# Four triangular inverses of a delta-rule layer: their 31 steps on GpSimd in place of VectorE

## The chip, the core and the metric

The kernel runs on one core of a Trainium2 chip. The metric is the device time of one execution in microseconds (us). Three runs of the kernel before gave 2785.96, 2793.25 and 2799.57 us, so a median of 2793.25 us.

## The reference

The program computes two blocks one after the other on 256 tokens of 1024 channels. The first is a stack of two layers, each with latent attention, a gated convolution, a sparse attention and a feed-forward network. The second block mixes differential attention with a delta-rule recurrence that runs over a context of 256 tokens and then over the 256 tokens themselves, forwards and backwards, in 16 heads of 64 channels; a feed-forward part of 16384 small experts follows. What the change touches is the recurrence. The reference writes it token by token:

```
def step(s, inp):
    w, kk, a, k, v, r = inp
    sa = jnp.einsum('dbhij,dbhj->dbhi', s, kk)
    s = s * w[..., None, :] - sa[..., :, None] * (kk * a)[..., None, :] + v[..., :, None] * k[..., None, :]
    return s, jnp.einsum('dbhij,dbhj->dbhi', s, r)
```

## The kernel before, in words

Every weight matrix is read in float32 pieces (tile `raw`, loads on the SP queue, line 304). ScalarE rounds a piece to `wh` (line 312), VectorE forms the rest `wl = raw - wh` (the subtraction helper, line 277), and TensorE multiplies with both halves (lines 333 to 335 and 351 to 353). This runs through nearly the whole program. There are three or four buffers of `wh` and `wl` each, so a split can be a few pieces ahead of the matmuls.

The recurrence is cut into chunks of 32 tokens. Inside a chunk the delta rule is a triangular system, and `wkv_front` inverts all its 32 x 32 matrices at once: 128 of them, one per partition (2 chunks of a pair, 2 directions, 32 combinations of pair and head). The function is called four times, once for each half of the heads and for context and tokens: in layer 1 and layer 2 of the first block beside the feed-forward network (for the context), in the second block beside the projections of the attention (tokens, first half) and beside the differential attention (tokens, second half). I call them the first to fourth inverse, and their places stretches 1 to 4.

One inverse goes like this. The masked products `ML` (tile `w8`) are stored in DRAM (`din`, lines 1313 and 1314) and loaded again with one matrix per partition as `Bt` (line 1316). `X` starts as minus the identity (memsets of lines 1318 and 1319). Then 31 steps follow, k = 0 to 30: a product of k+1 rows by 31-k columns into `tmp`, and its subtraction from `X`. Both are written with helpers, so that the profile shows them under line 271 (`mul`) and line 277 (`sub`), as tiles `w`; each step needs the one before it. `X` is stored (`dout`, line 1327) and loaded back in two layouts (lines 1331 and 1332), and the half that belongs to one direction is transposed on VectorE in 32 x 32 blocks (line 1333). First to use the inverse is the matmul of line 1392 in `wkv_back`, the part that runs through the chunks one after the other.

The order of the instructions of each engine is set when the program is built: a scheduler simulates the program with costs of its own and puts an instruction in its engine's queue where it expects its inputs to be there, calls of `wkv_front` and `wkv_back` ahead of other work that is ready. On the chip each queue then runs strictly in that order. An instruction whose input is late holds up all that stand behind it.

Of the kernel before, what the change touches and what calls it, by code (L numbers as in the profile page):

```python
# [15 lines left out]
ALU = mybir.AluOpType  # L16
# [178 lines left out]
class Kern:  # L195
# [980 lines left out]
    def wkv_front(self, pool, src, hf, zd, wa, own=False):  # L1176


        nc, C, P = self.nc, self.C, self.P2
# [135 lines left out]
        Bt = self.w4(pool, [128, 32, 32])  # L1315
        nc.sync.dma_start(Bt, din.rearrange("c d k r s -> (c d k) r s"))
        X = self.w4(pool, [128, 32, 32])
        nc.gpsimd.memset(X, 0.0)
        nc.vector.memset(X.rearrange("p a b -> p (a b)")[:, 0::33], -1.0)
        tmp = self.w4(pool, [128, 1024])  # L1320
        for k in range(31):
            n = 31 - k
            p = tmp[:, :(k + 1) * n].rearrange("p (c s) -> p c s", s=n)
            self.mul(p, X[:, 0:k + 1, k:k + 1].to_broadcast([128, k + 1, n]), Bt[:, k + 1:, k].unsqueeze(1).to_broadcast([128, k + 1, n]))
            self.sub(X[:, 0:k + 1, k + 1:], X[:, 0:k + 1, k + 1:], p)
        dout = self.t(self.dram, [2, 2, 32, 32, 32], "dout", bufs=2)
        nc.sync.dma_start(dout.rearrange("c d k r s -> (c d k) r s"), X)
        TB = self.w4(pool, [128, 32, 32])
# [624 lines left out]
```

## Time and profile before

| | |
|---|---|
| median of 3 runs | 2793.25 us |
| profiled execution | 2798.71 us, span 2796.9 us |
| TensorE busy | 2635.9 us, 94% of the span |
| VectorE busy | 1978.4 us, 71% |
| ScalarE busy | 1423.3 us, 51% |
| GpSimd busy | 14.2 us, 1% |

PE is TensorE's matmuls, PEld its weight loads, DVE is VectorE, ACT is ScalarE, POOL is GpSimd, SP issues the loads and stores. A busy share is a mean over stages that have different limits, so the four stretches of the inverses are read by themselves.

### The profile page before, as it was taken

The page shows a single profiled execution, that of the slowest core. Times are in us where ns is not written, and L with a number is a line of the kernel's source. Part 1 is how long each engine was busy: PE and PEld are TensorE (multiplying, and loading weights), DVE is VectorE, ACT ScalarE, POOL GpSimd, SP SyncE. Part 2 cuts the span into 40 slices and gives each one's busy share as a digit, 9 for nine tenths or more (in the row PEclk, how much of TensorE's full clock was granted, in tenths as well). Part 3 has the DMA queues.
Part 4 walks back from the last instruction along what each step waited for, and adds up shares of the span by engine and source line. Part 5 has one row for each costly group of instructions (what it writes and reads, how often), then busy time and mean ns, then how long its engine had stood idle before and what let it go on. Part 6 is the DMA issues. An engine that isn't in the chain of part 4 may idle for free.

```text
span 2796.9 us, 54976 instructions
## 1 busy us (share of the span) xinstructions
PE 2635.9 (94%) x21856; PEld 2293.4 (82%) x21856; DVE 1978.4 (71%) x4085; ACT 1423.3 (51%) x2392; POOL 14.2 (1%) x45
## 2 busy tenths in 40 slices
PE   7999899999999999987998979989989999999999
PEld 7986588886997768877888755779989998888887
DVE  5996668765897658766788776566987765666665
ACT  4554446543555446534664655444446554444444
POOL 0000000000000000000000000000000000000000
PEclk9999999999999999988999976699999999999999
DMA  5532866546543555535746522264664346666665
GB/s 189 175 124 88 263 225 199 168 152 219 167 147 126 162 199 170 173 107 166 237 134 200 166 68 59 67 200 163 190 185 137 122 149 208 215 208 219 207 216 183
DMA packets 212433, 472.00 MB, mean 169 GB/s; under 512 B 52816, under 2 KB 86480, under 8 KB 211152
## 3 DMA queue, kind: packets, MB, share of 16 engines
q1 hardware_dynamic: 212176, 468.48, 52.4%
q8 instruction: 172, 2.82, 0.4%
q14 instruction: 85, 0.70, 0.1%
HBM read 427.77 MB, written 40.63 MB: 167 GB/s over the span
## 4 chain that ended last, share of the span: by engine, by line
PE 79%; DVE 10%; DMA 6%; ACT 4%; issue 2%; SPq 0%; DVEq 0%; ACTq 0%
PE a L333 8%; PE a L335 8%; PE a L334 8%; PE b L353 4%; PE b L351 4%; PE b L352 4%; PE b L1767 3%; PE x L335 3%; PE x L333 3%; PE x L334 3%; PE a L352 3%; PE a L351 3%; PE a L353 3%; DVE wl L277 3%; DMA raw<-in_peer 2%
## 5 line engine op out<-in xcount | busy, mean ns | idle before, releaser
L312 ACT ACTIVATE wh<-raw 128x1024 fp32r<-128x1024 f32 (+1 forms) x701 | 638.2, 913 | 689.3 <-PE a L334 247.4
L277 DVE TENSOR_TENSOR wl<-raw,wh 128x1024 fp32r<-128x1024 f32 (+1 forms) x701 | 727.4, 1041 | 357.9 <-ACT wh L312 332.6
L333 PE MATMUL a<-hh,wh 128*128 128x256 f32 x1920 | 550.2, 287 | 8.8 <-ACT hh L1621 4.1
L335 PE MATMUL a<-hh,wl 128*128 128x256 f32 x1920 | 549.5, 286 | 4.5 <-DVE wl L277 4.2
L334 PE MATMUL a<-hl,wh 128*128 128x256 f32 x1920 | 547.2, 285 | 0.6 <-DVE hl L277 0.5
L333 PEld LDWEIGHTS a<-hh,wh 128*128 128x128 f32 x1920 | 365.5, 190 | 22.0 <-ACT wh L312 4.9
L335 PEld LDWEIGHTS a<-hh,wl 128*128 128x128 f32 x1920 | 365.2, 190 | 14.8 <-DVE wl L277 9.0
L334 PEld LDWEIGHTS a<-hl,wh 128*128 128x128 f32 x1920 | 364.9, 190 | 5.4 <-DVE hl L277 0.7
L333 PE MATMUL x<-hh,wh 128*128 128x256 f32 x720 | 205.8, 286 | 5.6 <-ACT wh L312 5.2
L335 PE MATMUL x<-hh,wl 128*128 128x256 f32 x720 | 206.6, 287 | 3.0 <-DVE wl L277 3.0
L334 PE MATMUL x<-hl,wh 128*128 128x256 f32 x720 | 204.9, 285 | 0.0
L352 PE MATMUL b<-wl,ah 128*128 128x512 f32 x512 | 201.0, 393 | 0.0
L351 PE MATMUL b<-wh,ah 128*128 128x512 f32 x512 | 191.2, 393 | 2.8 <-issue 2.8
L353 PE MATMUL b<-wh,al 128*128 128x512 f32 x512 | 191.8, 391 | 0.0
L333 PEld LDWEIGHTS x<-hh,wh 128*128 128x128 f32 x720 | 137.2, 191 | 9.0 <-ACT wh L312 6.7
L335 PEld LDWEIGHTS x<-hh,wl 128*128 128x128 f32 x720 | 136.9, 190 | 5.7 <-DVE wl L277 4.4
L1802 ACT ACTIVATE ah<-pact 128x256 fp32r<-128x256 f32 x128 | 52.6, 412 | 173.1 <-PE b L352 160.3
L334 PEld LDWEIGHTS x<-hl,wh 128*128 128x128 f32 x720 | 137.1, 190 | 0.8
L352 PE MATMUL a<-wl,hh 128*128 128x256 f32 (+2 forms) x416 | 128.6, 309 | 8.0 <-DVE wl L277 7.9
L351 PE MATMUL a<-wh,hh 128*128 128x256 f32 (+2 forms) x416 | 125.3, 308 | 6.2 <-DVE hl L395 3.9
L277 DVE TENSOR_TENSOR wl<-rawv,wh 128x1024 fp32r<-128x1024 f32 x84 | 101.7, 1222 | 37.1 <-ACT wh L312 37.0
L353 PE MATMUL a<-wh,hl 128*128 128x256 f32 (+2 forms) x416 | 125.9, 304 | 0.0
(672 smaller groups left out, 5436.7 us busy)
## 6 DMA issues: line engine op xcount, KB each, us to landing
raw<-in_flat SPq DMA_DIRECT2D x289, 512.0 KB, 4.0
raw<-in_peer SPq DMA_DIRECT2D x172, 512.0 KB, 3.9
raw<-in_flat SPq DMA_DIRECT2D x228, 256.0 KB, 3.6
rawv<-in_peer SPq DMA_DIRECT2D x84, 512.0 KB, 4.6
TG<-in_flat SPq DMA_DIRECT2D x52, 512.0 KB, 5.9
parked<-act SPq DMA_DIRECT2D x89, 128.0 KB, 2.1
pact<-parked SPq DMA_DIRECT2D x89, 128.0 KB, 4.5
w<-vtd SPq DMA_DIRECT2D x32, 128.0 KB, 4.1
```

Source lines behind the costliest of these rows:

```text
L277: self.nc.vector.tensor_tensor(out, a, b, op=ALU.subtract)
L312: self.nc.scalar.activation(h, src, AF.Copy)
L333: mm(ps, wh[:, k], xh[:, k], start=first and k == 0, stop=False)
L334: mm(ps, wh[:, k], xl[:, k], start=False, stop=False)
L335: mm(ps, wl[:, k], xh[:, k], start=False, stop=last and k == nk - 1)
L351: mm(ps, xh[:, k], wh[:, k], start=first and k == 0, stop=False)
L352: mm(ps, xh[:, k], wl[:, k], start=False, stop=False)
L353: self.last = mm(ps, xl[:, k], wh[:, k], start=False, stop=last and k == nk - 1)
L1767: nc.tensor.matmul(ps[:, c], a[:, n, g, :, c], b[:, g, :, c], start=n == 0, stop=n == 2)
L1802: nc.scalar.activation(ah, act, AF.Copy)
```

## The change

The memset of the diagonal and the two instructions of each of the 31 steps are issued on GpSimd. The formulas, the tiles and the transfers are the same.

```
         X = self.w4(pool, [128, 32, 32])
         nc.gpsimd.memset(X, 0.0)
-        nc.vector.memset(X.rearrange("p a b -> p (a b)")[:, 0::33], -1.0)
+        nc.gpsimd.memset(X.rearrange("p a b -> p (a b)")[:, 0::33], -1.0)
         tmp = self.w4(pool, [128, 1024])
         for k in range(31):
             n = 31 - k
             p = tmp[:, :(k + 1) * n].rearrange("p (c s) -> p c s", s=n)
-            self.mul(p, X[:, 0:k + 1, k:k + 1].to_broadcast([128, k + 1, n]), Bt[:, k + 1:, k].unsqueeze(1).to_broadcast([128, k + 1, n]))
-            self.sub(X[:, 0:k + 1, k + 1:], X[:, 0:k + 1, k + 1:], p)
+            nc.gpsimd.tensor_tensor(p, X[:, 0:k + 1, k:k + 1].to_broadcast([128, k + 1, n]), Bt[:, k + 1:, k].unsqueeze(1).to_broadcast([128, k + 1, n]), op=ALU.mult)
+            nc.gpsimd.tensor_tensor(X[:, 0:k + 1, k + 1:], X[:, 0:k + 1, k + 1:], p, op=ALU.subtract)
```

VectorE's queue at the start of the first inverse, before. Here `w_799` is `X`, `w_798` is `Bt`, `w_800` is `tmp`; `wl`, `mt` and `OL` belong to the feed-forward network:

```order
L1309 STREAM_TRANSPOSE w_796_4945<-w_787_4792 128x1024
L277 TENSOR_TENSOR wl_6009<-raw_6006,wh_6008 128x1024
L1319 MEMSET w_799_4954 128x32
L277 TENSOR_TENSOR wl_6027<-raw_6024,wh_6026 128x1024
L271 TENSOR_TENSOR mt_5981<-mt_5981 128x512
L271 TENSOR_TENSOR w_800_4957<-w_799_4954,w_798_4952 128x31
L277 TENSOR_TENSOR OL_5984<-mt_5981,OT_5983 128x512
L277 TENSOR_TENSOR w_799_4954<-w_799_4954,w_800_4957 128x31
L271 TENSOR_TENSOR w_800_4957<-w_799_4954,w_798_4952 128x60
```

The same steps in GpSimd's queue, now:

```order
L1318 MEMSET w_799_4954 128x1024
L1319 MEMSET w_799_4954 128x32
L1324 TENSOR_TENSOR w_800_4957<-w_799_4954,w_798_4952 128x31
L1325 TENSOR_TENSOR w_799_4954<-w_799_4954,w_800_4957 128x31
L1324 TENSOR_TENSOR w_800_4957<-w_799_4954,w_798_4952 128x60
L1325 TENSOR_TENSOR w_799_4954<-w_799_4954,w_800_4957 128x2x30
L1324 TENSOR_TENSOR w_800_4957<-w_799_4954,w_798_4952 128x87
L1325 TENSOR_TENSOR w_799_4954<-w_799_4954,w_800_4957 128x3x29
```

Nothing else stands between them there, and each waits for the one before it. VectorE's queue keeps the splits and the work of the other parts.

VectorE's queue where the first inverse has come back and is transposed, before (`w_799` in the first row is the last step's result, `w_802` the inverse loaded back):

```order
L277 TENSOR_TENSOR w_799_4954<-w_799_4954,w_800_4957 128x31
L277 TENSOR_TENSOR wl_6425<-raw_6422,wh_6424 128x1024
L277 TENSOR_TENSOR wl_6443<-raw_6440,wh_6442 128x1024
L271 TENSOR_TENSOR mt_6397<-mt_6397 128x512
L277 TENSOR_TENSOR OL_6400<-mt_6397,OT_6399 128x512
L277 TENSOR_TENSOR wl_6474<-raw_6471,wh_6473 128x1024
L1333 STREAM_TRANSPOSE w_787_4792<-w_802_5022 32x1024 x2
L277 TENSOR_TENSOR wl_6511<-raw_6508,wh_6510 128x1024
```

And now:

```order
L277 TENSOR_TENSOR wl_6407<-raw_6404,wh_6406 128x1024
L277 TENSOR_TENSOR wl_6425<-raw_6422,wh_6424 128x1024
L1333 STREAM_TRANSPOSE w_787_4792<-w_802_5022 32x1024 x2
L277 TENSOR_TENSOR wl_6443<-raw_6440,wh_6442 128x1024
L271 TENSOR_TENSOR mt_6397<-mt_6397 128x512
L277 TENSOR_TENSOR OL_6400<-mt_6397,OT_6399 128x512
```

The transposes have moved ahead of two weight splits (`wl_6443`, `wl_6474`) and the two instructions between them.

TensorE's queue at the first use of the first inverse (`w8_787` is `ML` with the inverse in it), before:

```order
L334 MATMUL a_974_6446<-hl_596_3540,wh_972_6442 128x256
L335 MATMUL a_974_6446<-hh_595_3539,wl_973_6443 128x256
L1392 MATMUL m_823_5261<-w8_803_5029,w8_787_4792 32x64
L333 MATMUL a_974_6446<-hh_595_3539,wh_972_6442 128x256
L334 MATMUL a_974_6446<-hl_596_3540,wh_972_6442 128x256
```

And now:

```order
L352 MATMUL a_861_5744<-wl_967_6407,OT_947_6295 128x512
L353 MATMUL a_861_5744<-wh_966_6406,OL_948_6296 128x512
L1392 MATMUL m_823_5261<-w8_803_5029,w8_787_4792 32x64
L351 MATMUL a_862_5745<-wh_966_6406,OT_947_6295 128x512
L352 MATMUL a_862_5745<-wl_967_6407,OT_947_6295 128x512
L353 MATMUL a_862_5745<-wh_966_6406,OL_948_6296 128x512
```

The first matmul of line 1392 has moved ahead of 33 weight matmuls, 21 of them 512 and 12 of them 256 columns wide. At the other three inverses it has moved ahead too: of 28 weight matmuls at the second (27 of 256 columns, one of 512), of 94 of 256 columns and four transposes at the third, and at the fourth from behind the transposes of `a_3030` to right behind those of `a_3020`, the ones that the trace shows at 1700.08 us; four matmuls of line 1499, two of line 1476 and four transposes stood between.

## Rows read from the trace of the kernel before

**Rows 1.** Busy time by stretch: length, then each engine (instructions), clock, DMA.

```profile
477.70:527.90 50.20, 50.20 (x503) 44.48 (x502) 46.21 (x87) 28.79 (x38) 0.00 (x0) 1.00 0.42 142
1104.70:1154.10 49.40, 49.40 (x506) 44.11 (x505) 45.48 (x86) 28.79 (x39) 0.00 (x0) 1.00 0.49 147
1448.50:1510.40 61.90, 51.05 (x488) 47.42 (x488) 56.28 (x152) 30.98 (x54) 0.00 (x0) 0.89 0.43 132
1657.40:1700.00 42.60, 28.16 (x251) 18.29 (x248) 41.46 (x111) 21.86 (x51) 0.00 (x0) 0.78 0.15 48
1660.00:1670.00 10.00, 1.44 (x28) 1.44 (x30) 9.83 (x24) 3.70 (x7) 0.00 (x0) 0.53 0.00 0
1670.00:1680.00 10.00, 9.30 (x100) 7.18 (x98) 9.93 (x30) 7.26 (x17) 0.00 (x0) 0.79 0.24 68
```

**Rows 2.** Groups of instructions of VectorE in stretch 1: busy us, mean ns, idle before.

```profile
L277 DVE TENSOR_TENSOR wl<-raw,wh 128x1024 fp32r<-128x1024 f32 x14 | 17.1, 1222 | 2.4 <-ACT wh L312 2.3
L271 DVE TENSOR_TENSOR w<-w,w 128x31 f32<-128x31 f32 (+15 forms) x31 | 15.0, 483 | 2.7 <-DMA w<-din 2.1
L277 DVE TENSOR_TENSOR w<-w,w 128x31 f32<-128x31 f32 (+15 forms) x31 | 10.6, 341 | 0.8
L277 DVE TENSOR_TENSOR OL<-mt,OT 128x512 fp32r<-128x512 f32 x4 | 2.7, 685 | 0.0
```

**Rows 3.** Waits in stretch 3: us in total, times, longest.

```profile
PE a L1108 <- DVE x L274: 4.9, 1, 4.9
PE a L352 <- DVE wl L277: 2.9, 5, 1.4
```

**Rows 4.** Waits from 1646 to 1700 us, around stretch 4.

```profile
PE a L1353 <- ACT w L268: 10.9, 1, 10.9
ACT w L1429 <- DVE w L277: 10.8, 1, 10.8
DVE w L271 <- DMA w<-din: 9.4, 1, 9.4
```

**Rows 5.** TensorE in order of time: start, duration, instruction (inverses 1, 3 and 4).

```profile
536.96 0.29 PE L1392 MATMUL m<-w,w 32*32 32x64 f32 x2
...
1518.40 0.29 PE L1392 MATMUL a<-w,w 32*32 32x64 f32 x2
...
1700.08 1.11 PE L1494 MATMUL a<-ident,x 128*128 128x128 f32 x4
...
1706.94 0.42 PE L1392 MATMUL a<-w,w 32*32 32x64 f32 x2
```

**Rows 6.** Groups of instructions of GpSimd over the whole span.

```profile
L642 POOL COPY P<-zk 128x256 f32<-128x256 f32 x4 | 2.0, 520 | 75.6 <-ACT zk L268 75.6
L1669 POOL CAST io<-consts 128x2048 bf16<-128x2048 f32 x1 | 1.9, 1890 | 207.3 <-DMA raw<-in_flat 207.3
...
L1753 POOL CAST io<-consts 128x512 bf16<-128x512 f32 x1 | 0.6, 614 | 109.5 <-PE x L335 109.5
```

**Rows 7.** VectorE in order of time: shortest and longest steps of inverse 1.

```profile
477.71 0.22 DVE L271 TENSOR_TENSOR w<-w,w 128x31 f32<-128x31 f32 x1 [2.06 <-DMA w<-din]
...
478.45 0.18 DVE L277 TENSOR_TENSOR w<-w,w 128x31 f32<-128x31 f32 x1
...
499.51 0.64 DVE L271 TENSOR_TENSOR w<-w,w 128x256 f32<-128x256 f32 x1
500.19 0.42 DVE L277 TENSOR_TENSOR w<-w,w 128x256 f32<-128x256 f32 x1
```

**Rows 8.** Order of time around 39 us: a weight split and GpSimd's copies.

```profile
38.90 1.23 DVE L277 TENSOR_TENSOR wl<-raw,wh 128x1024 fp32r<-128x1024 f32 x1 [2.28 <-ACT wh L312]
...
39.75 0.98 POOL L642 COPY P<-zk 128x256 f32<-128x256 f32 x2 [37.59 <-ACT zk L268]
```

**Rows 9.** TensorE in order of time: spacing of weight matmuls in stretch 1.

```profile
504.69 0.28 PE L335 MATMUL a<-hh,wl 128*128 128x256 f32 x1
504.80 0.40 PE L351 MATMUL a<-wh,OT 128*128 128x512 f32 x1
505.04 0.40 PE L352 MATMUL a<-wl,OT 128*128 128x512 f32 x1
```

## The prediction

> **What bounds the kernel now.** I read four views in turn. First the busy time in the four stretches in which the inverses run [rows 1]; the reader is to see that there are two kinds. In the first two stretches TensorE is busy for all of 50.2 and 49.4 us, at full granted clock, though VectorE is busy 92% of the time: TensorE sets the pace there, and VectorE freed of work gives nothing back. In the third and the fourth TensorE is idle for 10.9 and 14.4 us while VectorE is busy 91% and 97% of the time: there an inverse moved off VectorE could pay. Second the groups of VectorE's instructions in the first stretch [rows 2]: the 31 multiplications (15.0 us) and 31 subtractions (10.6 us) of the inverse share the engine with 14 weight splits of 1.22 us. Third, who waited in the third and fourth stretch [rows 3, 4]: in the third TensorE waits for a transpose's input (4.9 us) and for splits (2.9 us), in the fourth once for 10.9 us. That one goes back to VectorE, whose queue stands 9.4 us behind the inverse's first multiplication until its input has landed. Fourth, when TensorE first uses an inverse, the matmul of line 1392 [rows 5]: at 536.96, which is 9.1 us after the first inverse's end at 527.9 (store, two loads in other layouts, transposes between them), and 8.0 us after the third's.
>
> **What goes.** VectorE loses 4 x (15.0 + 10.6) = 102 us, a memset of 0.1 us per inverse, and the wait of its queue for the inverse's input. In stretches 1 and 2 that is worth 0 (no idle TensorE). In the third at most some 10 of the 10.9 us of idle TensorE, in the fourth the 10.9 us wait; so at best 21 us. The memset now stands on GpSimd, where it is hidden by the same wait for the input; without that cover it would cost 0.1 us.
>
> **What comes: the inverse's length on GpSimd.** One inverse is 62 instructions over 2 x 5456 = 10912 elements per partition (the sum of (k+1)(31-k), twice). No row shows a two-input instruction on GpSimd, so I bound it. The two casts [rows 6] differ by 1276 ns for 1536 elements: 0.83 ns an element and 0.19 us fixed; with the 0.04 us that dependent steps of the inverse stand apart on VectorE [rows 7] that is 0.23 us x 62 = 14.3 us fixed.
> - Low end, one pass at the cast's rate for both inputs: 14.3 + 10912 x 0.83 = 23.3 us.
> - High end, two passes at the copy's 520 ns for 256 elements [rows 6], 4.06 ns an element: 44.3 + 62 x 0.04 = 46.8 us.
> - Taken: two passes at the cast's rate, 1.66 ns, for the subtractions (9.1 us). For the multiplications, whose second operand is read at a stride of 32, I use VectorE's own ratio: between 31 and 256 elements the multiplication grows by 0.42 us, the subtraction by 0.24 [rows 7], a ratio of 1.75, so 2.9 ns and 15.8 us. Sum 39.2 us. This lies nearer the high end, because the copy, the row nearest to short rows and strides, is the slow one.
>
> **What both engines share.** In the first stretch at least 17.1 + 2.7 = 19.8 of 50.2 us (39%) are VectorE instructions that read two SBUF tensors [rows 2]. The one place that shows GpSimd reading beside such an instruction [rows 8]: a pair of copies that by the cast's line should take 2 x 0.40 us takes 0.98, having run 0.38 us beside a split; 0.18 us too much, about half of the overlap, if it is not just the copy's own rate. The split itself kept its 1.23 us. For an inverse, half of the overlap is 39.2 x 0.39 / 2 = 8 us; I take 12, as its instructions read two inputs where the copy read one. That makes 51 us for the first three inverses. In the fourth there are no weight splits; VectorE's other work is 41.5 - 25.6 = 16 of 42.6 us and only a part of it reads two tensors: I take 5, so 44 us.
>
> The Trainium skill (SBUF — State Buffer, "SBUF: two separate sides") says that VectorE and GpSimd hold one pair of SBUF ports exclusively, for a whole instruction, and that a VectorE instruction with two SBUF inputs blocks a GpSimd one that reads. The copies [rows 8] neither prove that nor exclude it; the first rival below is what it would do.
>
> **What is late then.** The scheduler has moved the users forward, as if the inverse were shorter than before. TensorE's first matmul of line 1392 stands before 33 matmuls (21 of 512 columns, 12 of 256) that it stood behind; at their spacing of 0.24 and 0.11 us [rows 9] that is 6.4 us. So the first inverse has to end 6.4 us before 527.9, which is 43.8 us after its start. The same count gives 3.2 us (28 matmuls, one of 512 columns) and 46.2 us for the second; 94 matmuls of 256 columns, 10.3 us and 51.6 us for the third. In the fourth the matmul now stands right behind the transposes at 1700.08, which end at 1701.2, so 5.7 us earlier than 1706.94; that leaves 36.9 us. What is beyond that, TensorE loses: its queue is in order, and behind the waiting matmul stand all later weight matmuls; on VectorE the two transposes of line 1333 hold the next splits back in the same way, and on SP the store of the inverse (line 1327) the next weight load. Below the limit nothing is won in the first two; in the third up to 10, in the fourth up to 10.9 us.
> - 1st: 51 - 43.8 = +7.2 us
> - 2nd: 51 - 46.2 = +4.8
> - 3rd: 51 - 51.6 = -0.6 (the 10 us that VectorE gives back are spent waiting)
> - 4th: 44 - 36.9 = +7.1 (its 10.9 us too)
> - Clock: behind the 10.9 us wait of before the granted clock was 0.53 and then 0.79 [rows 1], time partly at 1.2 GHz in place of 2.4; 10 us at 0.79 cost some 2 us. Two such stalls: +4.
>
> Sum +22.5, so +23 us, on the profiled execution's 2798.7 us 2822. The median of the runs shown, 2793.25, is 5 us lower, so I forecast 2816. My bounds move that: without any sharing and 23.3 us it is 0 + 0 - 10 - 10.9 = -21; without sharing and 46.8 us 3.0 + 0.6 - 4.8 + 9.9 = +9; with all the sharing see below.
>
> **Rivals.**
> 1. Full exclusion: the two engines never read together. An inverse then takes 39.2 / (1 - 0.39) = 64 us in the first three stretches and some 48 in the fourth: 20 + 18 + 12 + 11, and 8 of clock, +69: 2862. (This is the skill's rule of above; by its GPSIMD Engine Reference, "Engine selection", a two-input instruction takes about twice VectorE's time, which would make 51 us of the 25.6 even without exclusion, and nearly the forecast; no run here shows either yet.) For it: VectorE's work of this kind fills 39% of the stretch. Against it: the split beside the copies was not lengthened. Chance 0.17.
> 2. Faster: GpSimd takes both inputs at the rate of one and shares nothing that matters, 23 to 33 us an inverse. The place is the fourth stretch, the price TensorE's 10.9 us wait, which goes with VectorE's blocked queue, beside the 10 us of the third; it decides as soon as an inverse is shorter than 37 us, and is more than 14 us below 33 us. -21 at 23 us: 2772. For it: the casts are quick, and the wait is surely removed. Against it: two inputs, strides and short rows. Chance 0.17.
> 3. No difference: 33 to 48 us an inverse, the gain of the third stretch against the loss of the fourth. At 39.2 us without sharing -10 + 2.3, so -8: 2785; at 46.8 us +9: 2802. For it: the scheduler's places fit an inverse of that length. Chance 0.30.
>
> **How the numbers follow.** My forecast, 48 us and more with partial sharing, has 0.36, rival 1 0.17, rival 2 0.17, rival 3 0.30. About 0.5% (14 us) is what a measurement of this kernel can tell from no change. Faster by more: rival 2, 0.17. Within: rival 3, 0.30. Slower by more: 0.53. The likeliest case alone runs from 2808 (15 us lost) to 2845. The range for 8 in 10 takes in rival 3, most of rival 2 (an inverse down to 25 us) and most of rival 1: 2774 to 2875.
>
> **What will show it.** Right: 62 GpSimd instructions per inverse, spanning about 51 us from the landing of the input in the first three stretches; TensorE waiting 5 to 10 us before line 1392 in the first two stretches, where it waited for nothing; VectorE idle before line 1333; the fourth stretch without the 10.9 us wait before line 1353, but with a new one before line 1392. Wrong on the length: an inverse under 44 us, and no idle TensorE before line 1392. Wrong on the sharing: splits and GpSimd instructions of the same durations whether they overlap or not. Wrong on the lateness: a long inverse, and yet TensorE busy throughout. A difference that comes from stages without an inverse would refute the whole sum.

## The result, and the profile after

The changed kernel takes 2826.43 us (median of 4 runs, 2821.01 to 2829.05) against 2793.31 for the kernel before: 1.0117 times as long, 95% interval 1.0088 to 1.0146. That is 33 us slower; the forecast was 2816, slower by 23. The profiled execution has a span of 2827.3 us, 30.4 more than before.

Where the 30.4 us arose is seen from when each inverse's first step runs. The four stretches of the inverses after, in the columns of [rows 1] (length, then busy time of TensorE, its weight loads, VectorE, ScalarE and GpSimd, granted clock, DMA share, GB/s):

```profile
472.40:528.70 56.30, 52.41 (x519) 46.34 (x517) 29.34 (x25) 30.66 (x41) 51.51 (x62) 0.98 0.35 114
1115.10:1170.10 55.00, 54.23 (x522) 47.52 (x521) 28.30 (x24) 31.32 (x42) 50.22 (x62) 1.00 0.38 121
1468.30:1516.80 48.50, 40.02 (x413) 37.09 (x411) 35.48 (x59) 26.39 (x45) 43.72 (x62) 0.93 0.38 116
1681.90:1725.30 43.40, 37.01 (x309) 23.14 (x308) 27.69 (x53) 25.94 (x66) 38.52 (x62) 0.80 0.20 62
```

They begin 5.3 us earlier than before, then 10.4, 19.8 and 24.5 later (left ends against those of [rows 1]). So 15.7 us were lost from the first inverse to the second, 9.4 to the third, 4.7 to the fourth and 5.9 from there to the end; the 5.3 us gained ahead of the first lie where nothing was changed (VectorE, ScalarE and GpSimd work in the same order up to there) and are the difference between two executions. The inverses are 56.3, 55.0, 48.5 and 43.4 us long.

The groups of the first stretch, VectorE against [rows 2], and GpSimd's steps (busy us, mean ns, idle before):

```profile
L1324 POOL TENSOR_TENSOR w<-w,w 128x31 f32<-128x31 f32 (+15 forms) x31 | 28.1, 906 | 37.4 <-DMA w<-din 35.1
L1325 POOL TENSOR_TENSOR w<-w,w 128x31 f32<-128x31 f32 (+15 forms) x31 | 23.4, 756 | 2.4
L277 DVE TENSOR_TENSOR wl<-raw,wh 128x1024 fp32r<-128x1024 f32 x15 | 21.3, 1421 | 23.7 <-ACT wh L312 23.6
L271 DVE TENSOR_TENSOR mt<-mt 128x512 f32<-128x512 f32 x3 | 3.5, 1178 | 0.0
L277 DVE TENSOR_TENSOR OL<-mt,OT 128x512 fp32r<-128x512 f32 x3 | 3.1, 1037 | 0.1
```

VectorE now stands idle for 23.7 us before its splits, and yet each split takes 1.42 us instead of 1.22, and the instructions of 512 columns over 1.0 instead of 0.69. What stretches them shows in order of time (start, duration):

```profile
504.39 0.68 POOL L1325 TENSOR_TENSOR w<-w,w 128x252 f32<-128x252 f32 x1
505.16 1.65 POOL L1324 TENSOR_TENSOR w<-w,w 128x247 f32<-128x247 f32 x1
506.89 0.68 POOL L1325 TENSOR_TENSOR w<-w,w 128x247 f32<-128x247 f32 x1
...
504.56 1.60 DVE L277 TENSOR_TENSOR wl<-raw,wh 128x1024 fp32r<-128x1024 f32 x1
```

The split starts at 504.56 while GpSimd's subtraction runs until 505.07; it takes 0.38 us more than its 1.22, of the 0.51 us that it shares with the subtraction. GpSimd's next step starts at 505.16 and takes 1.65 us; its shortest execution of that size is 0.75. It ran its own 0.75 us only when the split was about done, at 506.16. Both fit one engine standing still until the other's instruction is done; the first experiment tests it.

What waited (us in total, times, longest): the first six rows are TensorE in stretches 1, 2, 3 (three rows) and 4, to be held against [rows 3, 4]; the last two are SP's queue and VectorE in stretch 1.

```profile
PE m L1392 <- DMA w<-dout: 10.7, 1, 10.7
PE x L1392 <- DMA w<-dout: 6.6, 1, 6.6
PE a L1108 <- DVE x L274: 5.5, 3, 3.8
PE a L352 <- DVE wl L277: 4.5, 2, 3.8
PE a L1392 <- DVE w L1333: 2.2, 1, 2.2
PE a L1392 <- DMA w<-dout: 5.2, 1, 5.2
SPq L1327 <- POOL w L1325: 13.0, 1, 13.0
DVE w L1333 <- DMA w<-dout: 13.2, 2, 12.6
```

TensorE, which before waited for nothing in the first two stretches, now waits for the inverse, right behind each of them. The 10.9 us of line 1353 in the fourth are gone (0.9 is left). And a wait costs more than its length, since the clock falls behind it. TensorE around the first one:

```profile
524.41 0.40 PE L353 MATMUL a<-wh,OL 128*128 128x512 f32 x1
535.50 0.39 PE L1392 MATMUL m<-w,w 32*32 32x64 f32 x2 [10.69 <-DMA w<-dout]
...
537.27 0.63 PE L351 MATMUL s<-wh,OT 128*128 128x512 f32 x1
537.69 0.63 PE L352 MATMUL s<-wl,OT 128*128 128x512 f32 x1
```

Weight matmuls of 512 columns stand 0.43 us apart until about 541, where [rows 9] has 0.24: the granted clock is 0.54 from 536 to 541, so near 1.2 GHz (before it was 1.00 from 536 to 541), which adds some 2.5 us. 10.7 + 2.5 is 13.2 of the 15.7 us. Another 1.9 lie in what TensorE waits between 575 and 720 us, at the stage's end: 7.2 us for the data of line 1035, against 5.3 before (3.4 there and 1.9 at line 424).

### The profile page after: what moved, and what is told of

Read it like the earlier page. It is cut to its first block, busy times and chain, and to the rows that moved or that the text cites. A ratio compares the mean times of both kernels' runs of the same rounds, so it can differ in the third digit from the quotient of the medians.

```text
span 2827.3 us, 54980 instructions
## 1 busy us (share of the span) xinstructions
PE 2642.9 (93%) x21856; PEld 2296.5 (81%) x21856; DVE 1922.2 (68%) x3833; ACT 1424.4 (50%) x2392; POOL 198.9 (7%) x297
## 4 chain that ended last, share of the span: by engine, by line
PE 75%; DVE 7%; DMA 6%; POOL 5%; ACT 4%; issue 3%; SPq 0%; DVEq 0%; ACTq 0%; POOLq 0%
PE a L333 8%; PE a L335 8%; PE a L334 8%; PE b L351 4%; PE b L352 4%; PE b L353 4%; PE b L1767 3%; PE x L335 3%; PE x L333 3%; PE x L334 3%; PE a L352 3%; POOL w L1324 3%; PE a L351 3%; PE a L353 2%; POOL w L1325 2%
## 5 line engine op out<-in xcount | busy, mean ns | idle before, releaser
L277 DVE TENSOR_TENSOR wl<-raw,wh 128x1024 fp32r<-128x1024 f32 (+1 forms) x701 | 738.6, 1058 | 409.2 <-ACT wh L312 389.2
```

The costliest lines, as they stand in the source:

```text
L277: self.nc.vector.tensor_tensor(out, a, b, op=ALU.subtract)
```

## The experiments

Theory A: an inverse on GpSimd is 39.7 us by itself; VectorE's instructions with two SBUF inputs shut it out and make it 55; TensorE stands at line 1392 in its in-order queue for what it is late. Rivals: GpSimd is that slow by itself (B), both engines slow down in proportion (C), the time is lost in stages without an inverse (D), a long inverse costs whatever its users do (E).

**The sharing by itself.** The network was left out; nine stretches of this run's own hold the 62 steps beside chosen work, or one of the two alone.

> The network is left out; what runs is the inverse's 62 steps on constant data, nine times, each beside other work: 1 GpSimd alone, 2 beside ScalarE's copies, 3 beside 16 weight splits on VectorE, one for each three ScalarE copies, 4 beside 40 splits back to back, 5 beside 16 VectorE instructions with one SBUF input, 6 beside 16 with one input in SBUF and one in PSUM, 7 the splits without GpSimd, 8 the inverse on VectorE alone, 9 an inverse on each engine at once. Theory A (an inverse is 39.7 us by itself, the sum of the shortest duration of each step in the changed kernel, 34.9 us, and 61 gaps of 0.078; each split holds GpSimd out for its whole 1.22 us): stretch 1 39 to 41 us, stretch 2 the same, stretch 3 52 to 58 us, stretch 4 over 80 us, stretch 6 39 to 42. Theory B (GpSimd is that slow by itself, sharing is minor): stretch 1 48 to 56 us, stretch 3 within 3 us of it. Theory C (both engines slow down in proportion, none is shut out): stretch 3 45 to 50 us, with the steps that overlap a split all stretched by the same factor. For stretch 5 the traces so far give nothing to go by: 40 us if only a second SBUF input shuts GpSimd out, over 50 if any long VectorE instruction does. The Trainium skill (SBUF - State Buffer, SBUF: two separate sides) says that also a one-input instruction in a two-port mode holds the shared ports, by which stretch 5 would be longer than 40 us.

Stretches 1, 2, 3, 4, 5, 6 and 9 (length, busy time of VectorE, ScalarE, GpSimd):

```profile
3.00:45.30 42.30, 0.00 (x1) 1.57 (x2) 35.04 (x62) 1.00 0.01 4
46.50:87.40 40.90, 0.00 (x0) 32.77 (x31) 35.22 (x62) 1.00 0.00 0
88.60:143.90 55.30, 22.45 (x16) 48.26 (x49) 49.51 (x62) 1.00 0.00 0
145.00:220.50 75.50, 62.87 (x41) 42.78 (x41) 69.64 (x62) 1.00 0.00 0
221.60:268.50 46.90, 12.67 (x16) 46.40 (x48) 41.18 (x62) 1.00 0.00 0
270.20:311.40 41.20, 9.12 (x14) 40.76 (x43) 35.28 (x62) 1.00 0.00 0
397.20:442.90 45.70, 42.88 (x64) 1.06 (x1) 39.84 (x62) 1.00 0.00 0
```

The steps alone are 35.0 us, with 61 gaps of 0.078 us 39.8; the rest of each length is one wait for ScalarE behind the first step, which belongs to the experiment. ScalarE's copies and VectorE's instructions with one operand in PSUM change nothing (35.2, 35.3). Sixteen splits lengthen GpSimd by 14.5 us, forty by 34.6. Theory A had over 80 us for stretch 4, which took 75.5: it had let GpSimd bear all of the waiting. The same kernel's groups: the splits of stretch 3, those without GpSimd, and the inverse on VectorE alone (busy us, mean ns):

```profile
L57 DVE TENSOR_TENSOR wl<-raw,wh 128x1024 fp32r<-128x1024 f32 x16 | 22.4, 1403 | 25.9 <-ACT wh L55 25.9
L57 DVE TENSOR_TENSOR wl<-raw,wh 128x1024 fp32r<-128x1024 f32 x10 | 12.2, 1225 | 18.1 <-ACT wh L55 18.1
...
L44 DVE TENSOR_TENSOR tmp<-X,Bt 128x31 f32<-128x31 f32 (+15 forms) x31 | 14.1, 456 | 1.1
L45 DVE TENSOR_TENSOR X<-X,tmp 128x31 f32<-128x31 f32 (+15 forms) x31 | 10.6, 342 | 2.0 <-ACT junk L38 0.9
```

Sixteen splits of 1.225 us are 19.6 us. GpSimd stands 14.5 of them, the splits 16 x 0.178 = 2.8, together 17.3; the remaining 2.3 fit into GpSimd's gaps. Of forty splits, 49.0 us, GpSimd stands 34.6 and the splits 16.8 (1.65 us each), 51.4 together, so about the whole of them. The splits of stretch 3 are not stretched alike either, as C would have it: they take from 1.22 to 1.84 us. So the two exclude each other; A holds but for the share that VectorE bears, B and C fall. This is the rule of the Trainium skill (SBUF — State Buffer, "SBUF: two separate sides"), the lock for a whole instruction, and this run agrees with it. In stretch 5 an instruction with one input in SBUF lengthens GpSimd by 6.1 us, less than the 11.1 us that the sixteen take by themselves.

**Half of the change.** `eng` is GpSimd where `not src` in the first kernel, `src` in the second, `own` in the third.

```diff
+        eng = nc.gpsimd if not src else nc.vector
+        eng.memset(X.rearrange("p a b -> p (a b)")[:, 0::33], -1.0)
...
+            eng.tensor_tensor(X[:, 0:k + 1, k + 1:], X[:, 0:k + 1, k + 1:], p, op=ALU.subtract)
```

> Only the first and second inverse on GpSimd, the third and fourth on VectorE as before. Theory A (the loss is the wait of TensorE's queue for the late inverse): slower than before by 18 to 22 us, the 10.8 and 8.3 us by which the changed kernel fell behind in these two stretches, with waits of about 10.7 and 6.6 us before line 1392's matmul, and third and fourth stretch as before. Theory D (the loss comes from stages without an inverse, by another order or other transfers): under 10 us here.

> Only the third and fourth inverse on GpSimd. Theory A: +4 to +9 us over before (the changed kernel fell behind by about 3 and 2 us in these stretches: gains of 4.5 us at line 1108 and of the 10.9 us wait at line 1353 are given back before and behind line 1392). Theory D: up to +20. Were it faster than before, the first two inverses would carry more than the whole loss.

> Only the fourth inverse on GpSimd. Theory A: the 10.9 us wait before line 1353 goes and comes back, in 5 us before line 1392 and in a chain of states that starts later: 0 to +6 us against before. Rival (the gain of the freed VectorE queue outweighs it where nothing else is moved): 5 to 10 us faster than before.

First two: 2832.3 us (5 runs), 1.0138 [1.0124, 1.0153], some 39 us slower than before, with TensorE's waits of 10.1 and 6.3 us as theory A has them, but far more than its 18 to 22 us. Last two: 2799.6 (12 runs), 1.002 [1.0007, 1.0033], 6 us slower. The fourth alone: 2798.4 (12 runs), 1.0026 [1.0012, 1.0040], 5.5 us, so the third by itself costs next to nothing. Both lie where theory A has them. The waits from 1630 to 1710 us with the fourth alone (the lines stand one further down):

```profile
PE a L1393 <- DMA w<-dout: 5.0, 1, 5.0
...
PE a L1354 <- ACT w L268: 1.6, 1, 1.6
```

The 10.9 us are down to 1.6, and 5.0 come back before the users. What makes it slower all the same isn't shown: the execution in the trace is the fastest of the twelve (2790.2 us). Most of the loss is in the first two stages, against D. But the parts don't add up: 39 + 6 is 45, the whole change 33. In the profile of the first two, TensorE's matmul of the same number ends 30.7 us later than before at 1600 us and 45.2 later at 1800, around the fourth inverse, which there is on VectorE as before. Nothing was edited there, yet the scheduler's order is another: from 1540 to 1816 us (by the kernel before) the instructions of VectorE and ScalarE other than the steps come in another order. So an edit to the first two inverses also reshuffles the work around the last two. Which place in that order takes these 15 us stays open.

**Without the splits.** In both feed-forward stages the subtraction is left out.

```diff
         with self.behind(act):
             self.nc.scalar.activation(h, src, AF.Copy)
+        if self.nolow:
+            return h, h
```

> The changed kernel without the subtraction that makes the low half of a weight split, in the two feed-forward stages only (the high half stands in for it in TensorE's products), so that VectorE runs almost nothing with two SBUF inputs beside the first two inverses. Only its trace is read, since it leaves work out. Theory A (39.7 us alone, plus about 1 us for each instruction of 512 that still shuts it out): inverses of 42 to 46 us instead of 56 and 55; line 1392's first matmul stands 3 + 30 and 23 + 4 matmuls earlier (some 4 and 6 us), so its waits fall from 10.7 and 6.6 us to 0 to 4. Theory B (GpSimd slow by itself): inverses over 50 us and waits as long as before.

> The partner of the run without the low half: the same subtractions are left out of the two feed-forward stages, but all four inverses stand on VectorE. The run with the inverses on GpSimd took 2787.4 us. Theory A (what makes the inverses cost in the first two stretches is that VectorE's splits shut them out of the port): without the splits only the third and fourth inverse still cost, the 6 us of the run with these two alone, so 2778 to 2785 here. Theory B (GpSimd costs there whatever VectorE does): the two lie some 33 us apart as the full kernels do, so 2750 to 2760 here.

The first two stretches with the inverses on GpSimd (columns as above):

```profile
469.10:512.00 42.90, 42.90 (x451) 37.27 (x450) 6.98 (x10) 26.06 (x36) 38.03 (x62) 1.00 0.41 139
1087.80:1130.10 42.30, 42.30 (x454) 37.45 (x453) 5.11 (x8) 25.40 (x36) 37.41 (x62) 1.00 0.46 139
```

And TensorE's only wait there from 480 to 575 us:

```profile
PE m L1396 <- DMA w<-dout: 0.5, 1, 0.5
```

The inverses shrink by 13 us to 42.9 and 42.3; 0.5 us of waiting is left at the first and none at the second. The one run took 2787.4 us; its partner with the inverses on VectorE 2791.9 (10 runs, 2784.7 to 2799.9). Both theories missed the partner's time: A had 2778 to 2785, for 6 us that the last two inverses should still cost, B 2750 to 2760. But instead of 33 us apart the two now cannot be told apart, as far as one run can tell. So the splits' exclusion makes the inverses late, and without the lateness there is no loss.

**Can the lateness be scheduled away?** Store, loads, transposes and users of the first two inverses were queued behind instructions of a later unit of the feed-forward stage; `finish` holds lines 1326 to 1333, and the last weight matmul, weight load and split traced so far are `lastpe`, `lastld` and `lastsub`. The last three kernels have (9, 13) for (7, 11).

```diff
+            if i == (7, 11)[l]:
+                with self.stream("n", "c"), self.tc.high_priority(offset=30000), self.behind(self.lastpe):
+                    with self.behind(self.lastld), self.behind(self.lastsub):
+                        self.finish()
+                    self.wkv_back(st, S)
+                    nc.sync.dma_start(self.Sd[l], S)
```

> All four inverses on GpSimd as in the changed kernel, but in the first two stretches the users (the store, the loads and transposes of lines 1327 to 1333, and all matmuls behind them) stand later in their queues: line 1392's first matmul 45 matmuls of 512 columns and 78 of 256 later in the first (some 20 us), 25 and 78 in the second (some 15 us). Theory A (only the lateness against the queue costs, not the length itself): the waits of 10.7 and 6.6 us go, and the time falls by 15 to 20 us against the changed kernel, to 2806 to 2812. Theory E (a long inverse costs by itself, since its port shuts VectorE's splits out and so starves TensorE): it stays at 2820 or above. If the held chain then ends behind its feed-forward stage, the second stretch gives some of it back.

2818.6 us (5 runs), 1.0086 [1.0072, 1.0099]: 8 us under the changed kernel's median, not 15 to 20. TensorE no longer waits at line 1392, but for weights (one row of the first stretch, two of the second), while SP's queue stands at the store (first stretch, second; lines stand up to nine further down in these kernels):

```profile
PE a L335 <- DVE wl L314: 3.3, 1, 3.3
PE a L333 <- ACT wh L312: 5.4, 1, 5.4
PE a L335 <- DVE wl L314: 4.6, 1, 4.6
SPq L1333 <- POOL w L1330: 9.5, 1, 9.5
SPq L1333 <- POOL w L1330: 16.1, 1, 16.1
```

So the store and the loads were given to GpSimd's own queue (`nc.gpsimd.dma_start` for the `dout` transfers), in the changed kernel and in the held one:

> The changed kernel with the inverse's store and the four loads behind it (lines 1327, 1331, 1332) issued from GpSimd's queue instead of SP's, where the store had stood 13.0 and 10.8 us (16.1 in the second stretch of the held kernel) in front of the weight loads. TensorE's first matmul of line 1392 stands nearly where it stood (7 matmuls of 512 columns later in the first stretch, 1 and 2 in the second). Theory A (TensorE's own place decides): the wait before line 1392 stays, 8 to 11 us in the first, 5 to 8 in the second, and the time stays within 5 us of the changed kernel's 2826. Theory S (SP's blocked queue takes the weights away and is what costs): 2805 to 2815.

> Both together: users held as in the held kernel (TensorE's first matmul of line 1392 the same 45 + 78 and 25 + 78 matmuls later) and the store and loads on GpSimd's queue, so that no weight load stands behind them. If the lateness against the two in-order queues, TensorE's and SP's, is the whole loss of the first two stretches (theories A and S together): no wait over 2 us before line 1392 or for weights there, and 17 to 21 us less than the changed kernel, 2805 to 2810. Theory E (an inverse of 56 us costs by itself, by VectorE's splits shut out of the port): not below 2816.

In the changed kernel it makes things worse, 2838.5 us (6 runs), 1.0162 [1.0137, 1.0187], where theory A allowed 5 us and theory S had a gain, and TensorE's waits in the two stretches are

```profile
PE m L1392 <- DMA w<-dout: 10.2, 1, 10.2
PE x L1392 <- DMA w<-dout: 9.9, 1, 9.9
```

SP no longer stands at the store, and TensorE's waits stay: its place in the queue makes them, not SP. What SP's waiting costs by itself this run can't price, since the transfers now come later. With both, 2821.8 us (5 runs), 1.0109 [1.0091, 1.0127], not 2805 to 2810: now VectorE stands at the transposes, and TensorE waits for splits (first stretch, second):

```profile
PE a L335 <- DVE wl L314: 5.6, 1, 5.6
PE a L335 <- DVE wl L314: 8.8, 1, 8.8
DVE w L1339 <- DMA w<-dout: 9.0, 2, 8.7
```

Three queues are in order, and an early place on any of them stops the weights. Then everything was held two units longer, with a control that has all inverses on VectorE:

> As the held kernel (store, loads, transposes and line 1392's matmuls back on their old queues, all held), but held two units of the feed-forward stage longer in both stages: TensorE's first matmul of line 1392 stands 48 + 96 matmuls behind its place in the held kernel, some 22 us, and 93 + 174 behind that of the changed kernel. In the held kernel SP still waited 9.5 and 16.1 us at the store and VectorE 5.9 us at the transposes, so that the weights came late; with 22 us more neither should wait. Theory A with S (an inverse costs only what its users wait for on the three in-order queues): no such wait on TensorE, SP or VectorE in the two stretches, and the 10.8 and 8.3 us of the changed kernel come back: 2803 to 2811. Theory E (the length itself costs): not below 2816, as in the two held kernels before. The chain of states then ends behind the second feed-forward stage, which may cost some us of it.

> The same holding, with only the first two inverses on GpSimd (third and fourth on VectorE), so against the kernel of that kind without holding, 2832 us. Theory A with S: 2793 to 2802, the time before or a few us more. Theory E: over 2815.

> The control: all four inverses on VectorE as before, with the same holding. It tells what the late place of the users costs by itself. Theory A with S: within 5 us of before, 2790 to 2799, since TensorE was never idle in these stretches. If it is slower than that, the held kernels pay for the place, not for the inverse.

Now TensorE waits for nothing from 480 to 600 us, and still: 2819.8 us (6 runs), 1.0111 [1.0093, 1.0129]; the first two alone 2831.0 (4 runs), 1.0136 [1.0115, 1.0157]; and the control, without any step on GpSimd, 2829.5 (5 runs), 1.0149 [1.0125, 1.0173]. So the late place costs by itself about what the late inverse cost, and my theory that holding would give the loss back is refuted. E's bound (not below 2816) was kept in these runs, but for another reason: at the same late place, the first two inverses on GpSimd (2831.0) and on VectorE (2829.5) cannot be told apart, so a long inverse costs nothing there. Where the time goes shows at the end of the first feed-forward stage. The last matmuls of the chain of states in the kernel before (count, duration, first and last start):

```profile
L1404 PE MATMUL x<-w,w x128: 218/218/267, 546.3 to 664.4; 64*64 64x64 f32 x128
```

The same matmuls in the control:

```profile
L1413 PE MATMUL x<-w,w x128: 218/218/366, 577.8 to 681.0; 64*64 64x64 f32 x128
```

Busy times from 640 to 700 us in the kernel before:

```profile
640.00:700.00 60.00, 54.76 (x414) 36.49 (x413) 30.65 (x68) 23.35 (x39) 0.72 (x3) 0.94 0.66 227
```

And in the control:

```profile
640.00:700.00 60.00, 49.88 (x530) 36.04 (x528) 31.19 (x78) 21.00 (x36) 0.72 (x3) 0.77 0.39 123
```

The last weight matmuls of the stage before, in the control and in the changed kernel, and the changed kernel's chain:

```profile
L353 PE MATMUL s<-wh,OL x57: 390/394/502, 479.6 to 665.8; 128*128 128x512 f32 x57
L353 PE MATMUL s<-wh,OL x57: 390/394/497, 480.3 to 657.3; 128*128 128x512 f32 x57
L353 PE MATMUL s<-wh,OL x56: 390/394/628, 484.7 to 674.7; 128*128 128x512 f32 x56
L1404 PE MATMUL x<-w,w x128: 218/218/267, 547.7 to 664.0; 64*64 64x64 f32 x128
```

Before, the chain's eight dependent rounds end at 664, with the stage. In the control they end at 681, when the stage's weight matmuls have been gone since 657: TensorE is idle for 10.1 instead of 5.2 of the 60 us, at a clock of 0.77 instead of 0.94. In the changed kernel it is the other way round: the users keep their early place, TensorE stands for them, the chain ends at 664 and the weight matmuls at 675.

All kernels side by side, from the traces: how many us the weight splits fell behind those of the kernel before in the first feed-forward stage (between the splits that start there at 445 and 799 us) and in the second (799 to 1350), and how long after the last weight matmul of each stage the chain ended.

| | behind, 1st | 2nd | chain's end, 1st | 2nd |
|---|---|---|---|---|
| before | | | -1.6 | 26.8 |
| changed | 15.8 | 7.9 | -10.9 | 24.2 |
| first two | 18.5 | 5.6 | -10.9 | 24.2 |
| changed, GpSimd's queue | 15.1 | 11.6 | -1.6 | 27.2 |
| held | 7.7 | 15.8 | 4.2 | 32.0 |
| held, GpSimd's queue | 11.0 | 5.9 | 4.6 | 31.5 |
| held longer | 13.3 | 9.0 | 23.6 | 44.4 |
| control | 14.1 | 8.8 | 23.6 | 44.4 |

The kernels with only the last two or the fourth inverse moved differ from the kernel before by up to 4.2 us in these columns, though their inverses there are as before. Most kernels lose 22 to 27 us over the two stages, by a wait where the users stand early and by a bare chain at the end (no weight matmuls of the stage beside it) where they stand late; the held one loses in the second stage what it saves in the first. Only the held one with GpSimd's queue loses less, 17 us. The second stage already ends with a bare chain in the kernel before. A place in between, at which the chain would end with the first stage and no queue would wait, was not tried, so that none exists is not shown. No complete version beat the kernel before.

## Why the prediction was right, and where its sizes were off

- **Length alone:** 39.2 us predicted, 39.8 measured. That it came so close is luck, as errors cancel: from 31 to 255 elements the shortest multiplication grows by 0.52 us, so 2.3 ns an element and not 2.9, the shortest subtraction by 0.43, so 1.9 and not 1.66; the fixed part is about 0.26 us with the gap, not 0.23.
- **Sharing, the mis-sized term:** +12, +12, +12 and +5 us were predicted, from "half of the overlap" in [rows 8]. Measured are 56.3, 55.0, 48.5 and 43.4 less 39.8: +16.5, +15.2, +8.7 and +3.6. Half of the overlap made 8 us, which I raised to 12 because the steps read two inputs; no row gave that figure. The mechanism was the first rival's, exclusion; that rival's price, 64 us, was too high, since VectorE runs beside the steps' gaps and bears part of the waiting itself. In the first stretch 15 splits and 6 instructions of 512 columns are 22.4 us at their durations of before; the 16.5 us are 0.74 of that, as 14.5 of 19.6 us in the run alone. I had given exclusion a chance of 0.17 because one split in [rows 8] was not lengthened; the split had started first, and it was the copies that took longer.
- **Twice VectorE's time:** the 51 us that the Trainium skill's two-input rule gave (GPSIMD Engine Reference, "Engine selection") is not what the run shows: alone the steps take 35.0 us against 24.7 on VectorE, 1.4 times. The measurement decides.
- **Lateness:** the limits of 43.8 and 46.2 us, from the matmuls that the users had moved ahead of, held. Lengths of 56.3 and 55.0 leave 12.5 and 8.8; TensorE waited 10.7 and 6.6, so they are good to some 2 us. The forecast's 7.2 and 4.8 were too small by the sharing.
- **Third and fourth:** -0.6 and +7.1 predicted; about 0 and 6 measured with these two alone, while in the whole change 4.7 us were lost from the third inverse to the fourth and 5.9 behind it. The fourth's wait before line 1353 went and another before line 1392 came, as said.
- **Clock:** 4 us were priced for two stalls; the first cost some 2.5.
- **Not seen:** that the users' early place was worth something. The sum priced the wait alone, as if it were pure loss; the held kernels show that a later place, which removes the wait, lets the chain of states end the stage later instead.
- **In all:** right were the path (a late inverse, and TensorE's queue in order behind it) and the signs named for it. The forecast was 10 us short, in part by the sharing in the first two stretches (3.5 and 1.8 us more waiting than it had). That its reason for the sharing was wrong cost it so little is luck too: the measured 56 us lie between its 51 and rival 1's 64.

## What to carry to other kernels

Work moved to GpSimd beside VectorE instructions that read two SBUF tensors takes its own time plus about three quarters of theirs (14.5 of 19.6 us here); GpSimd's low busy share does not show this, so add up the two busy times before moving. When a result comes later, look for the chain behind it, not only for who waits for it: holding the users back here mostly moved the loss to the end of the stage. And look at every in-order queue that its store, loads and users pass, DMA queues too.

## What the runs showed of the hardware

- A VectorE instruction with one SBUF input, 1024 columns in 0.69 us undisturbed, also holds GpSimd up: 16 of them cost it 6.1 us and took 0.83 us each. Beside instructions of 512 columns with the second operand in PSUM nothing is lengthened (0.69 us each, GpSimd 35.3).
- With an inverse on each engine at once, GpSimd's steps rose only from 35.0 to 39.8 us, VectorE's from 24.7 to 42.0: with short instructions it is VectorE that stands most.
- The transfers of an inverse issued from GpSimd took 0.8 us of that engine's time each, and TensorE's second wait for them was 9.9 us instead of 6.6.
